# A two-layer hybrid encoder trunk: retention values in seven wide products, sums of weights on VectorE, other transfers and pacing

## The chip, the cores and the metric

The kernel runs on one core of one Trainium2 chip. The metric is the device time of one execution in microseconds (us); lower is better. Engines are named as in the profile: PE is TensorE (matmul), PEld its weight loads, DVE is VectorE, ACT is ScalarE, POOL is GpSimd, SP is SyncE, which issues most of the weight loads. SBUF is the on-chip memory, PSUM the eight banks that TensorE writes.

## The reference

Inputs are x (1, 512, 1024), a per-layer embedding p, and weights of two layers. All of it is float32. Cut to what matters here:

```python
for i in range(DEPTH):                      # 2 layers
    h = rmsnorm(x, norm1_g[i])
    z = h @ w_in[i] + b_in[i]               # q/k/v/o/i/f of the mLSTM, q/k/v/g of the retention, two gates
    ...
    y_m = sigmoid(mo) * head_layernorm(mlstm(mq, mk, mv, ...), m_norm_g[i])
    rq4, rk4 = rope(rq), rope(rk) * R_DK ** -0.5      # 4 heads, dk = 256
    hr = retention(rq4, rk4, rv, log_gamma)           # rv: 4 heads, dv = 512
    y_r = silu(rg) * head_layernorm(hr, r_norm_g[i])
    x = x + (sigmoid(gm) * (y_m @ w_bm[i]) + sigmoid(gr) * (y_r @ w_br[i])) @ w_out[i]
    h2 = rmsnorm(x, norm2_g[i])
    x = x + square(relu(h2 @ w_ff1[i] + b_ff1[i])) @ w_ff2[i] + b_ff2[i]
    h3 = rmsnorm(x, norm3_g[i])
    x = x + sigmoid(h3 @ w_pe_gate[i]) * (p[i] @ w_pe[i])
return rmsnorm(x, final_g)
```

The retention of one head over 512 frames is computed as masked scores times values (`r_scores`, `r_attend`); the part of z that the change is about is rv, 2048 columns, 512 for each of four heads.

## The kernel before, in words

**Numbers.** Every float32 operand is split into a high part (ScalarE, a rounded copy, `split` L263) and a low part (VectorE, the difference, L264). A product takes three matmuls: high by high, high by low, low by high (`mm3` L378 to L380).

**Units.** Weights are streamed in units of 512 KB, in an order that `unit_list` writes out. A T8 unit is 128 output columns, 24 matmuls with 512 frames moving. A V unit is a quarter of 512 value columns: here the weights move and the activations stand, and four units make 96 matmuls 128x512 (`values`, L614, matmuls L630 to L632). A PAIR unit is 256 output columns by a Strassen-Winograd scheme: seven products of 12 matmuls 128x256 each, instead of eight (`run_pair`, L408; matmuls L427 to L429).

**A PAIR's pieces.** The products read three loaded pieces, A = (B11, t1), B = (B21, t2), C = (B22, t3), and a fourth, D = t4 = B21 + t2, that VectorE forms in B's raw buffer (L364). t1, t3 and t2 are sums of weight quarters that GpSimd's DMA queue forms in DRAM ahead of time, two steps each (copy, then accumulate), up to 1 MB each, for a group of up to four pairs (`sum_steps`, `step`, L308). The steps are issued at units given by `due` and each waits for a matmul of its time.

**Buffers.** `fill_raws` loads pieces into four raw buffers (a fifth while the retention stages last) from SP's queue; `prep_next` splits them, in order, into a ring of three high/low pairs (`PIECES`), and D into a ring of two. `READY` and `LOOK` say how far ahead of a product the pieces are prepared.

**PSUM of a pair.** Products P1, P6, P7 and P4 use bank "a", P2 "b", P5 and P3 "c". P1 is evacuated before P6 starts on "a", P6 before P7, P7 before P4. The order on TensorE is P1, P5, then P4 of the pair before (`flush`), P6, P2, P3, P7. In most stages ScalarE evacuates P1, P5, P6 and P4, and VectorE P2, P3 and P7 (`pair_tiles`, L455, L459, L461); in the feed-forward block all go to VectorE and are added to x there (L1215, L1217). A list scheduler fixes the final order on each engine; it may move instructions against the program's order.

**Retention stages.** For each head: `r_qk` (two pairs, then rope on VectorE, L936 to L938), `rv_vals`, `r_scores`, `r_attend`, head norm, and `r_out` (two gate pairs and transposes). `values` adds the bias on VectorE (L598) and splits the result (L612). Behind w_out, x is loaded again for the residual, from ScalarE's queue (L1165).

Of the kernel before, what the change touches and what calls it, by code (L numbers as in the profile page):

```python
# [35 lines left out]
F32 = mybir.dt.float32  # L36
F32R = mybir.dt.float32r
# [5 lines left out]
P = 128  # L43
T = 512
# [50 lines left out]
MADE = {"t1": ("B12", "B11"), "t3": ("B12", "B22"), "t2": ("t1", "B22")}  # L95
# [4 lines left out]
def due(k):  # L100

    return 3 + 7 * min(k, 15) // 4 + 9 * max(k - 15, 0) // 4


def groups():


    g = {}
    for i in range(L):
        def rqk(h):  # L110
            return [("w_in", 0, c + k * 256) for k in (h, h + 1) for c in (CRQ, CRK)]
# [12 lines left out]
    return g  # L124


def unit_list(i):
# [48 lines left out]
    v(CRV)  # L176
# [6 lines left out]
    v(CRV + 512)  # L183
    rg(0)
    rqk(2)
    v(CRV + 1024)
# [3 lines left out]
    v(CRV + 1536)  # L190
# [23 lines left out]
def build(ctx, tc, ins, out):  # L214
# [29 lines left out]
    bm_dram = tc.dram_tile([L, KT, P, T], F32, name="bm_spill")  # L244

# [27 lines left out]
    index, given, sums, k = {}, {}, {}, 0  # L273
    for g, v in groups().items():
        index[g] = len(index)
        for x in GIVEN:
            given[g, x] = ins["wpairs"][k:k + len(v)]
            k += len(v)
        for x in MADE:
            sums[g, x] = tc.dram_tile([len(v), P, Q], F32, name=f"s{index[g]}{x}")  # L280
# [7 lines left out]
    def sum_steps():  # L288

        first = lambda g: [(g, "t1", 0), (g, "t3", 0), (g, "t1", 1), (g, "t3", 1)]  # L290
        second = lambda g: [(g, "t2", 0), (g, "t2", 1)]
        gs = list(index)
        out = first(gs[0])
        for a, b in zip(gs, gs[1:]):
            f = first(b)
            for n, x in enumerate(second(a)):
                out += [x] + f[2 * n:2 * n + 2]
        return out + second(gs[-1])
# [12 lines left out]

    def next_unit():
        n = at["unit"]
        at["unit"] += 1
        while at["step"] < len(steps) and due(at["step"]) <= n:
            step()
        return n


    order = [(n, x) for n, u in enumerate(units) for x in (PIECE if u[0] == "PAIR" else (0,))]  # L320
    place = {x: k for k, x in enumerate(order)}
    loads = [(n, x) for n, x in order if x != "D"]
    raws, pieces = {}, {}
# [3 lines left out]
    at = {"unit": 0, "prep": 0, "load": 0, "whole": 0, "step": 0}  # L327

    def fill_raws(most=RAWS + 1):
        while at["load"] < len(loads) and len(raws) < most:  # L330
# [8 lines left out]
            if x:  # L339
                _, g, p = units[n]  # L340
                assert made[g] == 6, (g, made[g], at["unit"])
                for k, y in enumerate(PIECE[x]):
                    in_order("load", nc.sync.dma_start(r[:, k * Q:(k + 1) * Q], block(g, y)[p]))
            else:
                in_order("load", nc.sync.dma_start(r, ins["wstream"][at["whole"]]))
                at["whole"] += 1
            at["load"] += 1

    def prep_next():
# [8 lines left out]
        out_ = [pl.tile([P, w], F32R, name=f"w{a}{n}_{x}", **kw) for a in "hl"]  # L358
        r = raws.pop((n, "B" if x == "D" else x))
        in_order("prep", *split(r[:, :w], *out_))  # L360
        pieces[n, x] = out_
        if x == "B":

            ve.tensor_tensor(r[:, :Q], r[:, :Q], r[:, Q:], OP.add)  # L364
            raws[n, x] = r
# [42 lines left out]
    def run_pair(name, act, done):  # L408
# [33 lines left out]
        later.append(last)  # L442

# [352 lines left out]
    for i in range(L):  # L796
# [166 lines left out]
        def r_out(h, num, y):  # L963
            nm = f"l{i}r{h}o"
            gs = {}

            def gates(w):
                def consume(g):
                    for d in range(2):
                        ac.activation(g[d], g[d], AF.Silu, bias=bcol(i, "brg", 4 * h + 2 * w + d), scale=SIGN[d])  # L970
                        gs[2 * w + d] = g[d]

                return consume

            for w in range(2):
                pair_tiles(f"{nm}{w}", xs, gates(w))
# [41 lines left out]

        def rv_vals(h, mid=None):
            return values(i, f"l{i}r{h}", xn, None, bias_rows(1024 + h * 512), 1, mid)  # L1020
# [99 lines left out]
        vv = rv_vals(3)  # L1120
# [43 lines left out]
        for c in range(KT):  # L1164
            nc.scalar.dma_start(x[c], x_src[c])  # L1165
# [184 lines left out]
    assert at["unit"] == NU and at["prep"] == len(order) and not pieces and not raws and at["load"] == len(loads) and at["step"] == len(steps)  # L1350
# [3 lines left out]
def _pack_units(a):  # L1354
# [7 lines left out]
    for i in range(L):  # L1362
        for u in unit_list(i):
# [3 lines left out]
            elif u[0] == "PAIR":  # L1367
# [15 lines left out]
def _pack_pairs(a):  # L1383

    out = []
    for (i, _), g in groups().items():
# [3 lines left out]
    return np.ascontiguousarray(np.concatenate(out))  # L1390
# [73 lines left out]
```

## Time and profile before

| what | value |
|---|---|
| median of three runs | 2360.72 us |
| the three runs | 2360.53 to 2361.47 us |
| the profiled execution, its own time | 2361.21 us |
| its span from first to last instruction | 2359.5 us |
| bytes read and written in HBM | 396.72 and 134.22 MB |

The prediction shows lines of the profile. In the page's list of engines stand busy time, share of the span and number of instructions; in the 40 slices each digit is the busy share in tenths. A row of the timeline has start, duration, engine, line, operation, what it writes and reads, and in brackets how long the engine was idle before it and for whom. A row of the view of waits has the waiting instruction, whom it waited for, the sum in us, how often, and the longest. A row of groups has minimum, median and maximum duration in ns and the first and last start. Matmuls are pipelined, so their durations overlap; the step from one start to the next is what one costs.

### The profile page before, as it was taken

The numbers are of one execution on the slowest core, as the hardware profiler recorded it, in microseconds if no ns is written. First come the engines' busy times: TensorE is split into PE (matmuls) and PEld (weight loads), VectorE is DVE, ScalarE is ACT, GpSimd is POOL, SyncE is SP. The second block draws the span as 40 slices with busy tenths as digits, with TensorE's granted clock in tenths as the row PEclk, the third lists the DMA queues.
The fourth block names the chain that finished last, engine by engine and source line by source line (L and its number), as shares of the span: only waits on it lengthen the run. The fifth ranks groups of instructions, "written<-read, shape, count | busy, mean of one in ns | idle before, by whom it ended". The sixth has DMA issues, their size and how long they took to land. (4 is left out here: it accounts for less than half of the span.)

```text
span 2359.5 us, 35353 instructions
## 1 busy us (share of the span) xinstructions
PE 2341.2 (99%) x13788; PEld 2077.1 (88%) x13788; DVE 1623.0 (69%) x2511; ACT 1194.0 (51%) x1736; POOL 232.2 (10%) x340
## 2 busy tenths in 40 slices
PE   9999999999999999999999999999999999999998
PEld 7888898998998898899888888999989988998997
DVE  6877567774675677677768775677837656776675
ACT  5755344553553545445557563444526445455454
POOL 4111100000001100001311110000000010000012
PEclk9999999999999999999999999999999999999999
DMA  6655765557577666765665657756574853433441
GB/s 217 172 173 159 208 211 161 179 157 224 156 230 253 181 197 192 196 179 161 189 187 160 165 174 210 195 183 167 170 219 159 243 178 99 143 125 116 135 133 55
DMA packets 156263, 413.71 MB, mean 175 GB/s; under 512 B 15664, under 2 KB 18096, under 8 KB 156096
## 3 DMA queue, kind: packets, MB, share of 16 engines
q1 hardware_dynamic: 107568, 260.32, 33.2%
q0 software_dynamic: 31104, 119.55, 21.6%
q10 hardware_dynamic: 17424, 31.59, 3.8%
q8 instruction: 108, 1.77, 0.3%
q14 instruction: 59, 0.48, 0.1%
HBM read 396.72 MB, written 134.22 MB: 225 GB/s over the span
## 5 line engine op out<-in xcount | busy, mean ns | idle before, releaser
L263 ACT ACTIVATE wh<-wr 128x1024 fp32r<-128x1024 f32 x254 | 268.1, 1057 | 383.7 <-issue 64.1
L264 DVE TENSOR_TENSOR wl<-wr,wh 128x1024 fp32r<-128x1024 f32 x254 | 311.4, 1227 | 137.4 <-ACT wh L263 131.3
L263 ACT ACTIVATE wh_C<-wr 128x1024 fp32r<-128x1024 f32 x76 | 80.5, 1059 | 130.5 <-PE l0bm L379 13.0
L264 DVE TENSOR_TENSOR wl_B<-wr,wh_B 128x1024 fp32r<-128x1024 f32 x76 | 92.9, 1222 | 44.5 <-ACT wh_B L263 39.5
L263 ACT ACTIVATE wh_B<-wr 128x1024 fp32r<-128x1024 f32 x76 | 80.4, 1057 | 84.0 <-issue 15.2
L263 ACT ACTIVATE wh_A<-wr 128x1024 fp32r<-128x1024 f32 x76 | 80.1, 1054 | 76.3 <-PE l1f L379 11.3
L264 DVE TENSOR_TENSOR wl_A<-wr,wh_A 128x1024 fp32r<-128x1024 f32 x76 | 92.9, 1222 | 33.1 <-ACT wh_A L263 33.1
L264 DVE TENSOR_TENSOR wl_C<-wr,wh_C 128x1024 fp32r<-128x1024 f32 x76 | 92.8, 1221 | 17.3 <-ACT wh_C L263 17.3
L378 PE MATMUL l1f<-l1n2h,wh 128*128 128x512 f32 x256 | 99.8, 390 | 0.0
L378 PE MATMUL l0f<-l0n2h,wh 128*128 128x512 f32 x256 | 99.8, 390 | 0.0
L380 PE MATMUL l0f<-l0n2h,wl 128*128 128x512 f32 x256 | 99.7, 389 | 0.0
L380 PE MATMUL l1f<-l1n2h,wl 128*128 128x512 f32 x256 | 99.7, 389 | 0.0
L379 PE MATMUL l0f<-l0n2l,wh 128*128 128x512 f32 x256 | 99.6, 389 | 0.0
L379 PE MATMUL l1f<-l1n2l,wh 128*128 128x512 f32 x256 | 99.6, 389 | 0.0
L263 ACT ACTIVATE wh_D<-wr 128x512 fp32r<-128x512 f32 x76 | 47.6, 627 | 93.6 <-PE l1o32a L428 3.5
L264 DVE TENSOR_TENSOR wl_D<-wr,wh_D 128x512 fp32r<-128x512 f32 x76 | 52.1, 686 | 45.6 <-ACT wh_D L263 44.5
L380 PEld LDWEIGHTS l1f<-l1n2h,wl 128*128 128x128 f32 x256 | 48.0, 188 | 10.2
L380 PEld LDWEIGHTS l0f<-l0n2h,wl 128*128 128x128 f32 x256 | 48.0, 188 | 10.1
L378 PEld LDWEIGHTS l0f<-l0n2h,wh 128*128 128x128 f32 x256 | 48.1, 188 | 9.8
L378 PEld LDWEIGHTS l1f<-l1n2h,wh 128*128 128x128 f32 x256 | 48.1, 188 | 9.8
L379 PEld LDWEIGHTS l0f<-l0n2l,wh 128*128 128x128 f32 x256 | 48.1, 188 | 9.8
L379 PEld LDWEIGHTS l1f<-l1n2l,wh 128*128 128x128 f32 x256 | 48.1, 188 | 9.7
(5493 smaller groups left out, 8255.4 us busy)
## 6 DMA issues: line engine op xcount, KB each, us to landing
wr<-wstream SPq DMA_DIRECT2D x254, 512.0 KB, 4.6
wr<-wpairs SPq DMA_DIRECT2D x228, 256.0 KB, 3.5
s0t<-wpairs POOLq DMA_DIRECT2D x5, 1024.0 KB, 8.6
s2t<-wpairs POOLq DMA_DIRECT2D x5, 1024.0 KB, 8.4
s3t<-wpairs POOLq DMA_DIRECT2D x5, 1024.0 KB, 8.6
s4t<-wpairs POOLq DMA_DIRECT2D x5, 1024.0 KB, 8.5
s5t<-wpairs POOLq DMA_DIRECT2D x5, 1024.0 KB, 8.7
s6t<-wpairs POOLq DMA_DIRECT2D x5, 1024.0 KB, 9.0
```

The costliest lines, as they stand in the source:

```text
L263: a = ac.activation(hi_ap, src, AF.Copy)
L264: return a, ve.tensor_sub(lo_ap, src, hi_ap.bitcast(F32))
L378: te.matmul(o, sh, mh, start=first, stop=False)
L379: te.matmul(o, sh, ml, start=False, stop=False)
L380: cur["mm"] = te.matmul(o, sl, mh, start=False, stop=last)
```

## The change

1. **Retention values.** Two heads' values are made together as a unit WIDE (groups rv0 and rv2, `run_wide`): seven products of 24 matmuls 128x512 instead of 2 x 96. Weights move, in halves u0 and u1 of 512 KB; the activations are the operands that the pairs use already. There are 12 loads (B11, t1, t2, B21, t3, B22, two halves each), 14 splits, and t4 = t2 + B21 by VectorE, one instruction of 1024 columns for each half. Each product is evacuated by VectorE in two tiles. The first head's values are split at once; the second head's go to DRAM by GpSimd's queue (four of 256 KB) and are loaded again and split by `rv_load`.
2. **t2 of the pairs.** t2 = t1 + B22 is formed by VectorE in SBUF when piece C is prepared (76 instructions of 512 columns), not by DMA. The pieces are prepared in the order A, C, B, D; the raw buffer of A is kept until t2 is formed. A group of pairs needs four DMA steps instead of six, a pair five loads of 256 KB instead of six.
3. **Pace.** The DMA steps are issued by a credit that grows with each unit (`tick`) instead of by `due`.
4. **Order.** A head's first gate pair is pulled ahead into a place that the values had (`r_gates`).
5. **x.** The reload for the residual goes by GpSimd's queue instead of ScalarE's.

```diff
-PIECE = {"A": ("B11", "t1"), "B": ("B21", "t2"), "C": ("B22", "t3"), "D": ()}
+PIECE = {"A": ("B11", "t1"), "C": ("B22", "t3"), "B": ("B21",), "D": ()}
...
+WIDE = {"P1": ("B11", 0), "P5": ("t1", 4), "P6": ("t2", 5), "P2": ("B21", 2), "P7": ("t3", 3), "P3": ("B22", 6),
+        "P4": ("t4", 1)}
+
+TURNS = [(x, u) for x in ("P1", "P5") for u in range(2)] + [(x, u) for u in range(2) for x in ("P6", "P2")]
+TURNS += [(x, u) for x in ("P7", "P3", "P4") for u in range(2)]
+STEP, SHARE = 4.5, 0.7
+TIME = {"PAIR": (9.9, 3.9), "WIDE": (5.45, 2.7)}
...
-def due(k):
-
-    return 3 + 7 * min(k, 15) // 4 + 9 * max(k - 15, 0) // 4
...
+        g[i, "rv0"] = [("w_in", 0, CRV)]
+        g[i, "rv2"] = [("w_in", 0, CRV + 1024)]
...
-    v(CRV)
+    u.append(("WIDE", (i, "rv0"), 0))
     full("w_bm", 0, 0, 0, 4)
     rqk(0)
     for p in (2, 3):
         pair("gm", p - 2)
         full("w_bm", 0, 0, 2 * p, 2 * p + 2)
     rqk(1)
-    v(CRV + 512)
     rg(0)
+    u.append(("WIDE", (i, "rv2"), 0))
     rqk(2)
-    v(CRV + 1024)
     rg(1)
     rqk(3)
     full("w_br")
-    v(CRV + 1536)
     rg(2)
     rg(3)
...
+    def tick(kind=None):
+        t, load = TIME.get(kind, (5.45, 1.5))
+        at["credit"] += SHARE * t - load
+        while at["step"] < len(steps) and at["credit"] >= 0:
+            at["credit"] -= STEP * len(groups()[steps[at["step"]][0]]) / 4 if not is_wide(steps[at["step"]][0]) else STEP
+            step()
...
-        if x == "B":
+        if x == "A" or wide and x[0] == "t2":
+            kept[n, x] = r
+        elif x == "C":
+
+            ve.tensor_tensor(raws[n, "B"][:, Q:], kept.pop((n, "A"))[:, Q:], r[:, :Q], OP.add)
+        elif x == "B":
 
             ve.tensor_tensor(r[:, :Q], r[:, :Q], r[:, Q:], OP.add)
-            raws[n, x] = r
+            formed[n, "D"] = r
+        elif wide and x[0] == "B21":
+            t = cur["br"].tile([P, UN], F32, name=f"t4{n}_{x[1]}", tag=("ph", "pl")[x[1]])
+            ve.tensor_tensor(t, kept.pop((n, ("t2", x[1]))), r, OP.add)
+            formed[n, ("t4", x[1])] = t
...
+    def run_wide(name, act, done, mid=None):
...
+            b = {"P2": "b", "P5": "c", "P3": "c"}.get(x, "a")
+            first = x in ("P1", "P2", "P5")
+            if first and u == 0:
+                bank[b] = [ps(f"{name}{b}{t}") for t in range(2)]
+            ready(place[n, (y, u)] + LOOK)
+            wh, wl = pieces.pop((n, (y, u)))
+            for k in (2 * u, 2 * u + 1):
+                h, l = act[k](j)
+                s = slice(k % 2 * T, (k % 2 + 1) * T)
+                f, e = first and k == 0, k == 3
+                for t in range(2):
+                    ts = slice(t * P, (t + 1) * P)
+                    o = bank[b][t]
+                    te.matmul(o, h[:, ts], wh[:, s], start=f, stop=False, skip_group_check=True)
+                    te.matmul(o, h[:, ts], wl[:, s], start=False, stop=False, skip_group_check=True)
+                    cur["mm"] = te.matmul(o, l[:, ts], wh[:, s], start=False, stop=e, skip_group_check=True)
+            if u:
+                for t in range(2):
+                    done(x, t, bank[b][t])
...
+        def rv_load(h):
+
+            v = value_tiles(f"l{i}r{h}")
+            for j in range(NT):
+                t = tmp(f"l{i}r{h}vr{j}")
+                gp.dma_start(t, rv_dram[i, h // 2, j])
+                split(t, v[0][j][:, :T], v[1][j][:, :T])
+            return v
...
         num = r_attend(0, pt, vv)
-        vv = rv_vals(1)
+        gs = {}
+        r_gates(0, 0, gs)
+        vv = rv_load(1)
         pt = r_scores(1, qk)
         yr = acts(cur["br"], f"l{i}yr0")
-        r_out(0, num, yr)
+        r_out(0, num, yr, gs)
         num = r_attend(1, pt, vv)
+        vv = rv_vals(2)
         qk = r_qk(2)
-        vv = rv_vals(2)
+        gs = {}
+        r_gates(1, 0, gs)
         pt = r_scores(2, qk)
-        r_out(1, num, yr)
+        r_out(1, num, yr, gs)
...
-        vv = rv_vals(3)
+        vv = rv_load(3)
...
-            nc.scalar.dma_start(x[c], x_src[c])
+            gp.dma_start(x[c], x_src[c])
```

More of the change, by code (lines that the diff above doesn't have):

```diff
@@ L288, in sum_steps @@
     def sum_steps():
[L290 to L298, printed above, removed]
+        out = []
+        for g in index:
+            out += [(g, "t1", 0), (g, "t3", 0), (g, "t1", 1), (g, "t3", 1)]
+            if is_wide(g):
+                out += [(g, "t2", 0), (g, "t2", 1)]
+        return out
     steps = sum_steps()
@@ L1349, in build @@
     x_pool.release()
-    assert at["unit"] == NU and at["prep"] == len(order) and not pieces and not raws and at["load"] == len(loads) and at["step"] == len(steps)
+    assert at["unit"] == NU and at["prep"] == len(order) and not pieces and not raws and at["load"] == len(loads) and not kept and not formed and at["step"] == len(steps)
 def _pack_units(a):
@@ L1366, in _pack_units @@
                 put(a[nm][i, r:r + D, c:c + P])
-            elif u[0] == "PAIR":
+            elif u[0] in ("PAIR", "WIDE"):
                 continue
```

136 lines of the change are left out of this document (104 added, 32 removed).

## The prediction

> **What bounds the kernel now.** I read the page first, for the share of each engine and whether it changes along the span, then the clock, the view of waits for TensorE, and single stretches in the timeline.
>
> ```profile
> span 2359.5 us, 35353 instructions
> PE 2341.2 (99%) x13788; PEld 2077.1 (88%) x13788; DVE 1623.0 (69%) x2511; ACT 1194.0 (51%) x1736; POOL 232.2 (10%) x340
> PE   9999999999999999999999999999999999999998
> DVE  6877567774675677677768775677837656776675
> core 0: 2359.5 us, clock 0.998
> ```
>
> TensorE is busy in every slice, at a granted clock of 0.998. The other engines are not near their limits on average, but VectorE stands at 7 or 8 tenths in many slices. What TensorE waits for is little:
>
> ```profile
> PE l0o33a L427 <- DVE l0x L1217: 2.0, 2, 1.5
> PE l1o33a L427 <- DVE l1x L1217: 2.0, 2, 1.5
> PE l1n41rp L572 <- DVE l1n41d L570: 1.6, 1, 1.6
> PE l0m0vp L631 <- DVE wl L264: 1.4, 1, 1.4
> PE warm L786 <- POOL ones_r L252: 1.1, 1, 1.1
> ```
>
> These rows and the smaller ones behind them come to about 10 us in 2359. So the time is the sum of TensorE's matmuls, and a change counts by the matmuls that it removes less the new gaps that it opens. The retention values, pairs of the feed-forward product and the retention stages all run without a gap now, which is why each new wait costs its full length.
>
> **What is removed.** The values of two retention heads take 2 x 96 matmuls of 512 columns before, and 7 x 24 = 168 of the same form after: 24 fewer for each of four pairs of heads, 96 in all. The instruction order shows nothing else leaving TensorE.
>
> ```profile
> L630 PE MATMUL l0r1vp<-wh,l0xnh x32: 389/389/389, 387.1 to 408.2; 128*128 128x512 f32 x32
> ```
>
> This row is every third matmul of one head. From its first to its last start there are 31 steps of three, 93 matmuls in 21.1 us: 0.227 us each (389 ns is the overlapping, modelled duration). 96 x 0.227 = 21.8 us. [...]
>
> **What VectorE is given.** Its pitches, from neighbouring starts:
>
> ```profile
> 939.15 1.22 DVE L264 TENSOR_TENSOR wl_B<-wr,wh_B 128x1024 fp32r<-128x1024 f32 x1 [0.55 <-ACT wh_B L263]
> 940.29 0.41 DVE L1217 TENSOR_TENSOR l0x<-l0x,l0o11c 128x256 f32<-128x256 f32 x1
> 940.63 0.68 DVE L364 TENSOR_TENSOR wr<-wr 128x512 f32<-128x512 f32 x1
> 941.23 0.41 DVE L1217 TENSOR_TENSOR l0x<-l0x,l0o11a 128x256 f32<-128x256 f32 x1
> 941.93 1.22 DVE L264 TENSOR_TENSOR wl_C<-wr,wh_C 128x1024 fp32r<-128x1024 f32 x1 [0.29 <-ACT wh_C L263]
> 943.08 0.41 DVE L1217 TENSOR_TENSOR l0x<-l0x,l0o12a 128x256 f32<-128x256 f32 x1
> 940.84 1.06 ACT L263 ACTIVATE wh_C<-wr 128x1024 fp32r<-128x1024 f32 x1 [1.72 <-PE l0o11a L428]
> 940.75 0.28 PE L427 MATMUL l0o12a<-l0hh,wh_A 128*128 128x256 f32 x1
> 943.58 0.28 PE L427 MATMUL l0o11a<-l0hh,wh_D 128*128 128x256 f32 x1
> ```
>
> A split of 1024 columns takes 1.14, a sum of 512 takes 0.60, an evacuation of 256 takes 0.34. New are 76 sums t2 (45.6 us). A wide unit has 14 splits and two t4 sums of 1024 columns, 14 evacuations and four value splits of 512: 16 x 1.14 + 18 x 0.60 = 29.0 us, and the reloaded head's four splits elsewhere are 2.4; before, two heads took 8 x 1.14 + 16 x 0.60 = 18.7. Four pairs of heads: 4 x 12.7 = 51 us. With these 97 us VectorE goes from 69% to about 73%: no new bound by its mean. What matters is where these instructions stand in its queue.
>
> **The new wait between two pairs.** In the rows above a pair (l0o12) starts at 940.75, call it 0. Piece C of the new pair takes the buffer that P7 of the old pair has just left, so ScalarE's wh_C starts at 0.09 and wl_C at 1.18. Before, the evacuations of the old P3 and P7 (940.29 and 941.23) stand ahead of wl_C. The old pair's P4, at 2.83 (943.58), writes the same PSUM bank as P7, so it needs that evacuation. In the changed order, piece C is prepared second and wl_C stands ahead of the old P3 and P7 evacuations on VectorE. Then: wl_C 1.18, evacuations at 2.33 and 2.67, the latter's end 2.67 + 0.41 = 3.08, P4 at 3.11 (0.03 is the step from wh_C's end to wl_C) instead of 2.83: 0.28. Next late is wl_B, 3.01 to 4.23, and behind it the evacuation of the new P1, 4.15 to 4.56; P6 shares P1's bank and wanted 3.11 + 1.41 = 4.52: 0.07 more. Together 0.35 us for each pair-to-pair change of this kind. Where the next t2 sum also stands between wl_C and the P7 evacuation, 0.60 is added, and the sum is about 1.0.
>
> Following the changed order for a layer's feed-forward blocks: of nine changes from pair to pair in blocks 0 to 2, three have the P7 evacuation early enough (0), five are of the first kind (1.75), one (second to third pair of block 0) is of the second (1.0). Block 3, where VectorE is already what TensorE waits for (the l0o33a row), I put at 0. That is 2.75 us per layer. Between pairs with a T8 unit in between (merge gates) P4 is late anyway and the cover is 2.7 us of T8 matmuls: 0; without them each would cost 0.35.
>
> **The retention stages.** Before, they ran at these shares:
>
> ```profile
> core 0: us, PE busy (x) PEld busy (x) DVE busy (x) ACT busy (x) POOL busy (x), PEclk, DMA share, GB/s
> 387.00:408.40 21.40, 21.40 (x96) 17.72 (x95) 12.37 (x22) 5.67 (x7) 3.03 (x4) 1.00 0.63 178
> 409.00:460.00 51.00, 51.00 (x395) 49.38 (x394) 39.94 (x67) 31.36 (x52) 2.48 (x4) 1.00 0.50 163
> ```
>
> The value unit (first stretch, 58% of VectorE) was the place where rope and norm work could catch up; the pair stage (78%) was the dense one. After, the values of heads 1 and 3 are not there to catch up in, and a wide unit of 168 x 0.227 = 38.1 us itself wants 29 us. The pair stretch from r_qk(2) to r_qk(3) has, counted in the changed order, 61 us of VectorE in 73 us of TensorE. By hand, per layer: the chain r_qk(0) to the second gm pair 2.0 (t2 stands waiting for piece C's load, 3.5 us or more after the slot is freed); r_qk(1) 0.35; P4 of the first gate pair behind head 0's norm and rope 0.6; r_qk(2)'s first change 0.8; the scores of head 2 waiting for the last k split 0.8; P4 of the last r_gates(1) pair 0.8 (between 0 and 1.6, as wl_C comes before or after P7's end); r_qk(3) 0.3; r_gates(2), where the scores, four value splits and a t2 precede the evacuations, 1.1; r_gates(3) 0.6; the two wide units 0.5 each. Sum 8.35. Each lies between 0, if the queue runs a little ahead, and about double. Places that I did not follow, and the second layer's own order: 0 to 2 us per layer, taken as 1, since nothing there can shorten TensorE's work.
>
> **Transfers.**
>
> ```profile
> wr<-wstream SPq DMA_DIRECT2D x254, 512.0 KB, 4.6
> wr<-wpairs SPq DMA_DIRECT2D x228, 256.0 KB, 3.5
> s2t<-wpairs POOLq DMA_DIRECT2D x5, 1024.0 KB, 8.4
> q0 software_dynamic: 31104, 119.55, 21.6%
> L1165 ACTq DMA_DIRECT2D l0x<-xT x8: 335/339/412, 719.1 to 734.5; - x8
> L308 POOL DMA_DIRECT2D s9t<-wpairs x5: 548/869/905, 823.1 to 951.2; - x5
> ```
>
> A wide unit loads 12 x 512 KB in 38 us, one per 3.2 us against 4.6 to land with four or more buffers: hidden; with only one buffer ahead it would cost 1.4 a piece. Groups of pairs need four DMA steps instead of six, so the pacing has room: by the code the last step of any group is issued at least five units (27 us or more) ahead of its first use, against some 9 us that a 1 MB step takes; 0. The eight reloads of x go behind each other on GpSimd, eight issues of 0.9 = 7 us instead of 0.34 each, ahead of the eight evacuations of w_out, which come 5.44 us apart (24 x 0.227): hidden, else about 5 us per layer. Spills and reloads of the second head have some 30 us: 0. [...]
>
> **Sum.** Per layer 2.75 + 8.35 + 1 = 12.1; two layers 24.2. Against the profiled execution: 2359.5 - 21.8 + 24.2 = 2361.9 span, plus the 1.7 between its span and its time (2361.21); that execution is 0.5 above the median of 2360.72, so about 2363 for the median. The whole saving is given back.
>
> **Rivals.** (1) *The waits stay covered*, and only the feed-forward changes remain, which follow from rows alone: 2 x 2.75, plus 3 for the rest. 2360.7 - 21.8 + 8.5 = 2347. For it: the stretch at 78% ran without a gap. Against: its evacuations stood ahead of the splits. (2) *VectorE becomes the bound in the wide units*, slower: 29 us of its own work and 8 to 12 of norm and rope of the neighbouring head meet in 38 us; above 38, each wide unit's splits come late turn after turn, as the ring of three pieces allows no lead. At 42 a wide unit costs 4 more, 16 for four: 2363 + 16 = 2379. It decides from a VectorE share of about 95% there. (3) *The matmuls saved are not saved time*: if the pitch of the wide unit were longer than 0.227 because weights change every four rows. Four units have 672; at 0.01 us more for each, 6.7 is not saved: 2370. Against: form and order of three per product are those of the values before.
>
> **How the numbers follow.** Forecast 0.5 (2354 to 2373), rival 1 0.25, rival 2 0.15, rival 3 0.05, others (a late sum or reload, slower) 0.05. About 0.2%, 4.7 us, is what a measurement can tell: below 2356 is faster, above 2365.4 slower. Rival 1 and a little of the forecast give faster 0.3; of the forecast, about 0.27 lies within; the rest, with rivals 2 and 3, slower 0.43, as unseen waits only add. Range: from rival 1's 2347 to rival 2's 2379.
>
> **What would show it.** TensorE instructions fall by 96, pitch in the wide unit 0.227. In the view of waits the new rows are first matmuls of P4 and P6 (tiles ending in "a") waiting for VectorE, 0.3 to 1 us each, some 30 us in all instead of 10. VectorE's share about 73%. Under 18 us in such rows makes rival 1 right; gaps inside the wide tiles, waiting for wl, make rival 2 right; waits for a DMA at piece loads, x or sums prove the part on transfers wrong.

## The result and the profile after

The changed kernel takes 2356.67 us (median of 20 runs, 2354.59 to 2359.66); the kernel before took 2361.14 us in the runs beside it (20 runs, 2360.43 to 2361.96). The ratio is 0.9982 (0.9976 to 0.9988): 4.5 us faster. Forecast were 2363 us and a range of 2347 to 2379. The time lies in the range, but the kernel became faster and not slower. Of the 21.8 us that the 96 matmuls are worth, 17.3 are given back, not 24.2.

From the page of the kernel after (span; engines with busy time, share and instructions; TensorE's tenths of 40 slices; clock):

```profile
span 2356.1 us, 35296 instructions
PE 2328.2 (99%) x13692; PEld 2062.1 (88%) x13692; DVE 1716.9 (73%) x2643; ACT 1217.9 (52%) x1760; POOL 252.3 (11%) x372
PE   9999999999999999999999999999999999999998
core 0: 2356.1 us, clock 0.997
```

13788 matmuls have become 13692, and VectorE stands at 73%, both as forecast. The slices show no gap. But the busy time of TensorE fell by 13.0 us (2341.2 to 2328.2), not by 21.8. Matmul records overlap, so this difference is no exact sum, but it suggests that something besides waiting got slower. The view of waits for TensorE, kernel after (who waited, for whom, total us, times, longest):

```profile
PE l0r2o1a L472 <- ACT wh_A L286: 4.4, 1, 4.4
...
PE l0r1brqa L472 <- DVE l0r1brqy L539: 1.4, 1, 1.4
...
PE l0r0o0a L472 <- DVE l0r0o0y L539: 1.2, 1, 1.2
```

All rows of this view add up to 20.5 us, against 11.5 before. One new row is far longer than any other: the second gate pair of head 2 in layer 0, waiting for piece A, and it has no counterpart in layer 1. To place the rest I took the step from each matmul's start to the next one's in the timeline, less 0.227 us for one of 512 columns and 0.118 for one of 256 (other widths in proportion), and summed this excess by the tile ahead of the step, before and after. The differences come to 18.2 us, against 18.4 from the spans (2359.5 - 21.8 = 2337.7; 2356.1 - 2337.7):

| place | excess, us |
|---|---|
| l0r2o, the pairs with the 4.4 us wait, layer 0 | +8.1 |
| P4 of the first gate pair of head 0, two layers | +2.8 |
| pitch inside the four wide units | +2.6 |
| l0r1br, q pair of head 1, layer 0 | +1.8 |
| first tile of bank c in a wide unit of layer 0 | +1.3 |
| l1r2o, layer 1 | +0.9 |
| l0m3, an mLSTM stage | +0.8 |
| feed-forward blocks 0 to 2, both layers, 0.1 to 0.4 at a place (l0o11 +0.3) | +2.0 |
| feed-forward block 3, both layers (l0o31 +1.0, l0o32 and l1o32 -0.8 each, the rest small) | -1.2 |
| all other places together | -0.9 |

**The 4.4 us wait.** The timeline of the kernel after, GpSimd, the ScalarE queue and ScalarE, then TensorE (start, duration, operation, in brackets the idle time before it and the releaser):

```profile
591.79 0.90 POOL L331 DMA_DIRECT2D s8t<-wpairs  x1 [9.98 <-DMA br_spill<-l0brs]
592.44 1.94 POOL L1147 DMA_DIRECT2D l0r3vr<-rv_spill  x3
602.05 0.54 POOL L1147 DMA_DIRECT2D l0r3vr<-rv_spill  x1 [7.67 <-issue]
592.74 0.33 ACTq L1252 DMA_DIRECT2D br_spill<-l0brs  x1
607.72 0.63 ACT L286 ACTIVATE l0r3vh<-l0r3vr 128x512 fp32r<-128x512 f32 x1 [1.88 <-DMA l0r3vr<-rv_spill]
608.26 1.04 ACT L286 ACTIVATE wh_A<-wr 128x1024 fp32r<-128x1024 f32 x1
609.35 0.55 PE L472 MATMUL l0r2o1a<-l0xnh,wh_A 128*128 128x256 f32 x1 [4.41 <-ACT wh_A L286]
```

Read it backwards. The matmul waits for wh_A, and wh_A stands on ScalarE behind the split of the fourth reloaded value tile. That tile was loaded only from 602.05, 7.67 us after the other three, and its row names no releaser ("issue"). In GpSimd's queue the four reloads stand behind a step of the sums (s8t, 1 MB). For that step and for the reloads, the view of their source line answers:

```profile
L331 POOL DMA_DIRECT2D s8t<-wpairs x1: 897/897/897, 591.8 to 591.8; - x1
DMA to landing us min/median/max: 9.9/9.9/9.9
L1147 POOL DMA_DIRECT2D l0r3vr<-rv_spill x4: 541/794/854, 592.4 to 602.1; - x4
DMA to landing us min/median/max: 5.6/10.7/11.6
```

591.79 + 9.95 = 601.74: the step lands, and 0.31 us later the last reload is issued. The same 0.31 to 0.32 stands between the two in each of the four other runs below that keep the reload on GpSimd's queue behind this step. By these runs it is not a buffer that it waits for. `rv_load` takes its temporaries from the six that `full("w_br")` spills from (l0brs), and the seventh of its eight spills, issued at 592.74 and slow too (8.8 us), also lands just ahead, at 601.5. But in the run with t2 by DMA the seventh spill lands at 599.2, the step at 607.91, and the last reload is issued at 608.22. In layer 1 no steps are left to issue by then, and there is no wait. The windows around the wait (us, busy us and count of PE, PEld, DVE, ACT, POOL, granted clock, DMA share, GB/s):

```profile
600.00:604.00 4.00, 4.00 (x36) 4.00 (x35) 1.90 (x3) 1.47 (x3) 1.10 (x2) 1.00 1.03 384
613.00:616.00 3.00, 3.00 (x16) 3.00 (x15) 1.52 (x2) 1.33 (x2) 0.00 (x0) 0.50 0.24 87
```

After the wait TensorE runs at a clock of 0.50 until about 616: 16 matmuls in 3 us, against 36 in 4 us ahead of it. The trace's record of the clock has 0.50 from 609.4 to 616.2. These 6.8 us do the work of 3.4: 28 matmuls of 256 columns start in them, 3.3 us at 0.118 each, and where nothing waits their step is 0.213. So the stall costs 4.4 + 3.4 = 7.8 of the 8.1 us at l0r2o, and this is where part of TensorE's busy time stayed. The page's mean clock, 0.997 after 0.998, hides it.

**The feed-forward change that came only in part.** The same change from l0o11 to l0o12 that the prediction counted out, timeline of the kernel after:

```profile
942.33 1.06 ACT L286 ACTIVATE wh_C<-wr 128x1024 fp32r<-128x1024 f32 x1 [1.11 <-issue]
943.42 1.22 DVE L287 TENSOR_TENSOR wl_C<-wr,wh_C 128x1024 fp32r<-128x1024 f32 x1
944.56 0.41 DVE L1350 TENSOR_TENSOR l0x<-l0x,l0o11c 128x256 f32<-128x256 f32 x1
945.22 0.42 DVE L1350 TENSOR_TENSOR l0x<-l0x,l0o11a 128x256 f32<-128x256 f32 x1 [0.24 <-PE l0o11a L474]
945.02 0.28 PE L472 MATMUL l0o12a<-l0hh,wh_A 128*128 128x256 f32 x1
947.85 0.28 PE L472 MATMUL l0o11a<-l0hh,wh_D 128*128 128x256 f32 x1
947.81 1.23 DVE L287 TENSOR_TENSOR wl_B<-wr,wh_B 128x1024 fp32r<-128x1024 f32 x1 [2.17 <-ACT wh_B L286]
948.96 0.42 DVE L1350 TENSOR_TENSOR l0x<-l0x,l0o12a 128x256 f32<-128x256 f32 x1
949.52 0.36 PE L472 MATMUL l0o12a<-l0hh,wh_B 128*128 128x256 f32 x1
```

And the first matmul of P6 in the kernel before, where the new pair starts at 940.75:

```profile
944.99 0.28 PE L427 MATMUL l0o12a<-l0hh,wh_B 128*128 128x256 f32 x1
```

wl_C does stand ahead of the evacuations of P3 and P7, as the instruction order had it. But wh_C starts at 942.33, before the new pair begins (945.02), because C, prepared second now, takes a buffer that came free earlier. VectorE is idle when P7 ends, the evacuation starts at 945.22, and P4 comes 2.83 us after the new pair's start, as before the change. The last link of the chain did come: wl_B goes ahead of the evacuation of the new P1, and P6, which needs P1's bank, starts 4.50 us after the new pair instead of 4.24. With the step behind it that is the 0.3 at l0o11.

### The profile page after: what moved, and what is told of

The parts are those of the page before. It is cut to its first block, busy times and chain, and to the rows that moved or that the text cites. A ratio compares the mean times of both kernels' runs of the same rounds, so it can differ in the third digit from the quotient of the medians.

```text
span 2356.1 us, 35296 instructions
## 1 busy us (share of the span) xinstructions
PE 2328.2 (99%) x13692; PEld 2062.1 (88%) x13692; DVE 1716.9 (73%) x2643; ACT 1217.9 (52%) x1760; POOL 252.3 (11%) x372
## 5 line engine op out<-in xcount | busy, mean ns | idle before, releaser
L286 ACT ACTIVATE wh<-wr 128x1024 fp32r<-128x1024 f32 x222 | 234.0, 1055 | 298.3 <-issue 64.9
L287 DVE TENSOR_TENSOR wl<-wr,wh 128x1024 fp32r<-128x1024 f32 x222 | 273.6, 1233 | 94.1 <-ACT wh L286 93.8
L286 ACT ACTIVATE wh_B<-wr 128x1024 fp32r<-128x1024 f32 x100 | 105.9, 1059 | 158.1 <-PE l0f L424 8.5
L287 DVE TENSOR_TENSOR wl_B<-wr,wh_B 128x1024 fp32r<-128x1024 f32 x100 | 122.1, 1221 | 31.0 <-ACT wh_B L286 30.8
L287 DVE TENSOR_TENSOR wl_A<-wr,wh_A 128x1024 fp32r<-128x1024 f32 x76 | 92.8, 1221 | 17.2 <-ACT wh_A L286 16.7
L402 DVE TENSOR_TENSOR wr<-wr,wr 128x512 f32<-128x512 f32 x76 | 52.2, 687 | 16.0 <-DMA wr<-wpairs 14.4
L425 PEld LDWEIGHTS l0f<-l0n2h,wl 128*128 128x128 f32 x256 | 48.0, 188 | 10.2
L425 PEld LDWEIGHTS l1f<-l1n2h,wl 128*128 128x128 f32 x256 | 48.0, 188 | 10.2
```

The lines of the kernel that those rows point to most:

```text
L286: a = ac.activation(hi_ap, src, AF.Copy)
L287: return a, ve.tensor_sub(lo_ap, src, hi_ap.bitcast(F32))
L402: ve.tensor_tensor(raws[n, "B"][:, Q:], kept.pop((n, "A"))[:, Q:], r[:, :Q], OP.add)
L425: cur["mm"] = te.matmul(o, sl, mh, start=False, stop=last)
```

## The experiments

Each edit is against the kernel after, unless it says otherwise. Ratios are to the kernel before, with 95% intervals.

**Reload by another queue.** Two kernels move the reload of the second head's values off GpSimd's queue, one to SyncE's, one to ScalarE's (the second has `nc.scalar` in the same place).

```diff
-                gp.dma_start(t, rv_dram[i, h // 2, j])
+                nc.sync.dma_start(t, rv_dram[i, h // 2, j])
```

> The second head's values are loaded again by SyncE's queue instead of GpSimd's; everything else as changed. Theory (queue): in layer 0 the reload of head 3 stands behind a 1 MB sum step in GpSimd's queue, lands 8 to 10 us after its issue, and ScalarE, in order, holds wh_A of the next gate pair behind it; that costs some 7 us on TensorE in the gate pairs of head 2 of layer 0 (excess over the matmuls' pitch 8.4 us there in layer 0 against 1.2 in layer 1). Then the time falls by 6 to 8 us, to about 2349.5, the 4.4 us wait is gone, and layer 1 is unchanged. Rival (work): the four extra splits and the second t2 sum in that place cost the time, whatever the queue: within 1.5 us of the changed kernel. A second rival: SyncE's queue then holds the weight loads behind the reload's own wait and new waits for wh or wl appear: slower than the changed kernel.

> The second head's values are loaded again by ScalarE's queue instead of GpSimd's. Theory (queue): the same gain as from SyncE's queue, 6 to 8 us, unless ScalarE's issue waits for the buffers that the spills of w_br leave; then ScalarE holds wh of a weight unit and 1 to 5 us come back. Rival (work): within 1.5 us of the changed kernel.

SyncE's queue: 2358.29 us, 0.9989 (0.9979 to 0.9999); ScalarE's: 2358.02 us, 0.9990 (0.9981 to 0.9999). Neither beats the change. The wait is still there, in each kernel's view of waits; on SyncE's queue:

```profile
PE l0r2o1a L472 <- ACT wh_A L286: 4.7, 1, 4.7
```

On SyncE's queue the four reloads are issued from 596.1 to 602.0 and take 8.6 to 8.8 us to land, beside the same step. On ScalarE's they are issued from 596.5 to 602.9, the last behind the split of the first, and the wait is 5.7, with another of 1.5 in layer 1. So another queue alone does not help. It does not clear GpSimd's queue in the kernel after: there the last reload is issued when the step has landed.

**No sum step beside the spills.** `tick` issues nothing during the eight w_br units of heads 0 and 1 (row block 0) and the unit behind them.

```diff
+        n = at["unit"] - 1
+        if any(units[m][0] == "T8" and units[m][1] == "w_br" and units[m][2] == 0 for m in (n, n - 1)):
+            return
```

> No sum step is issued during the eight w_br units of heads 0 and 1; the credit goes on and the steps come behind them. Buffers as in the changed kernel. Theory (DMA engines shared with a sum step): the spills land in 2 to 4 us as in layer 1, the last reload is issued some 5 us earlier, and layer 0's gate pairs of head 2 lose at most 2 us as in layer 1: 2349 to 2352. Rival (buffers alone, or work): the wait of 4.4 us stays, within 2 us of 2356.7.

2355.87 us, 0.9981 (0.9972 to 0.9991): no better than the change within the interval. Its reloads, the seventh spill, and its view of waits:

```profile
L1150 POOL DMA_DIRECT2D l0r3vr<-rv_spill x4: 536/554/606, 573.7 to 589.9; - x4
DMA to landing us min/median/max: 2.7/2.9/3.0
L1255 ACTq DMA_DIRECT2D br_spill<-l0brs x1: 326/326/326, 592.6 to 592.6; - x1
PE l0r2o1a L475 <- DVE l0r2o1y L542: 3.0, 1, 3.0
PE l0r3o1a L477 <- DVE wl_A L287: 1.9, 1, 1.9
```

The wait for wh_A is gone. The reloads are issued 12 to 19 us earlier, the last one ahead of the seventh spill (so it does not need that spill's buffer), and land in 3 us instead of 5.6 to 11.6. So the steps made the reload late: ahead of it in GpSimd's queue, and as a transfer beside it. But the steps held back now come behind each other, and two waits for VectorE stand at 623.5 and 643.9 us instead of the one at 609.4. After the 3.0 us wait the granted clock stays at 1.00.

**Reload into its own buffers.** The reload goes straight into the value tiles (the low part, split in place), and head 3's is issued ahead of `full("w_br")`. So no buffer is shared with the spills, and the reload goes ahead of the steps that stood ahead of it. The recorded texts call this kernel e6.

```diff
-                t = tmp(f"l{i}r{h}vr{j}")
-                gp.dma_start(t, rv_dram[i, h // 2, j])
-                split(t, v[0][j][:, :T], v[1][j][:, :T])
+                gp.dma_start(v[1][j][:, :T].bitcast(F32), rv_dram[i, h // 2, j])
+            return v
+
+        def rv_split(v):
+            for j in range(NT):
+                split(v[1][j][:, :T].bitcast(F32), v[0][j][:, :T], v[1][j][:, :T])
...
-        vv = rv_load(1)
+        vv = rv_split(rv_load(1))
...
+        vv = rv_load(3)
         for c in range(KT):
...
-        vv = rv_load(3)
+        vv = rv_split(vv)
```

> The reloaded head's values land in the value buffers themselves (the low part's, split in place), not in the six temporaries that the spills of w_br also use, and head 3's reload is issued before w_br. Moving the reload to another queue had changed nothing: the last reload was issued at 602.0 in both, just after a w_br spill that shared the DMA engines with a 1 MB sum step (issued at 591.8) had taken 8.8 us. Theory (shared temporaries): the reload then lands long before the scores of head 3, the 4.4 us wait of layer 0 and the half clock behind it go (7 to 8 us), and layer 1 stays: 2348 to 2350. Rival (work): the splits and sums that stand ahead on ScalarE and VectorE hold the gate pair: within 2 us of 2356.7.

2352.09 us (2350.11 to 2353.69), 0.9965 (0.9953 to 0.9978): 4.6 us below the change, faster than both kernels. Its issues in the view of the source line, and its window over the place of the stall:

```profile
L1146 POOL DMA_DIRECT2D l0r3vl<-rv_spill x4: 546/558/594, 532.6 to 534.7; - x4
```

```profile
604.00:616.00 12.00, 12.00 (x104) 12.00 (x103) 7.45 (x12) 7.02 (x13) 0.00 (x0) 1.00 0.61 206
```

The reloads are issued 60 us earlier, TensorE runs through at full clock, and the excess at l0r2o goes back to what it was before the change. The run does not separate the buffers from the earlier issue. The span falls by 5.5 (2356.1 to 2350.6) and not by 8. Two of the places that give some back are in its view of waits, where the kernel after had 1.2 each:

```profile
PE l0r0o0a L472 <- DVE l0r0o0y L539: 1.7, 1, 1.7
PE l1r0o0a L472 <- DVE l1r0o0y L539: 1.7, 1, 1.7
```

**Piece buffers strictly in turn.** This makes the prediction's assumption true: piece C of the new pair gets exactly the buffer that P7 of the old pair leaves.

```diff
-        out_ = [pl.tile([P, w], F32R, name=f"w{a}{n}_{nm}", **kw) for a in "hl"]
+        if kw["tag"] == "w":
+            turn = at["turn"] = at.get("turn", -1) + 1
+            out_ = [pl.tile([P, w], F32R, name=f"w{a}{n}_{nm}", tag=f"w{turn % PIECES}{a}", bufs=1) for a in "hl"]
```

> The three buffer pairs of the split pieces are taken strictly in turn, so that piece C of a pair must take the buffer of the last pair's piece C and wait for its P7, as the prediction assumed; in the changed kernel wh_C started at 942.33, before P7 (943.61 to 945.02) had begun. Theory (buffers): the prediction's chain then appears, about 0.35 us at each of some ten feed-forward changes from pair to pair and about 1 us at two of them, 5 to 6 us in all, and some more in the retention stages: 2361 to 2366 us. Rival: the chain is covered in any case, for example because the evacuation of P7 runs earlier than I chained it: within 1.5 us of the changed kernel's 2356.7.

2356.87 us, 0.9983 (0.9974 to 0.9992): no different. The same change of pairs in its timeline:

```profile
945.18 0.42 DVE L1354 TENSOR_TENSOR l0x<-l0x,l0o11a 128x256 f32<-128x256 f32 x1 [0.99 <-PE l0o11a L478]
946.21 1.23 DVE L287 TENSOR_TENSOR wl_C<-wr,wh_C 128x1024 fp32r<-128x1024 f32 x1 [0.60 <-ACT wh_C L286]
```

C does wait for P7 now, but the scheduler then puts the P7 evacuation ahead of wl_C. Where the buffer is late the order is the harmless one, and where the order is the harmful one the buffer is early. The order and the buffer were not independent, and the chain that joined them, through P7 to P4, does not stand at this change of pairs in either kernel.

**t2 formed later.** t2 is formed just ahead of B's split, so that it does not stand waiting for C's load.

```diff
         if x == "B":
+            ve.tensor_tensor(r[:, Q:], kept.pop((n, "A"))[:, Q:], kept.pop((n, "C"))[:, :Q], OP.add)
...
-
-            ve.tensor_tensor(raws[n, "B"][:, Q:], kept.pop((n, "A"))[:, Q:], r[:, :Q], OP.add)
+            kept[n, "C"] = r
```

> VectorE forms t2 just before piece B is split, not when piece C is prepared; pieces A and C keep their raw buffers until then. Theory: the t2 sum no longer stands ahead of wl_C and the evacuations while it waits for a load (4.09 us at the second pair of r_qk(1), layer 0), so the 1.4 us there and the 0.9 in layer 0's last feed-forward block go: 2 to 3 us less than 2356.7. Rival: two raw buffers are kept instead of one, so loads start later and weight splits wait: 2 to 10 us more, with new waits for wl or wh.

2359.80 us, 0.9998 (0.9988 to 1.0007): 3.1 slower than the change. The place aimed at did improve (l0r1br by 1.7), and l0r0o, l1r0o (1.5 each) and the merge gates of both layers got worse.

**t2 of the pairs by DMA again**, with all else as in the change, the pieces in the old order A, B, C, D, and the credit of a step cut to two thirds.

```diff
-PIECE = {"A": ("B11", "t1"), "C": ("B22", "t3"), "B": ("B21",), "D": ()}
+PIECE = {"A": ("B11", "t1"), "B": ("B21", "t2"), "C": ("B22", "t3"), "D": ()}
...
-            if is_wide(g):
-                out += [(g, "t2", 0), (g, "t2", 1)]
+            out += [(g, "t2", 0), (g, "t2", 1)]
```

> The pairs' t2 is formed by DMA steps again, with the pieces in the order A, B, C, D, six steps per group and the same credit per group; the wide units and everything else stay. Theory: of the 17.5 us given back, the t2 sums on VectorE hold about 3 (1.6 at the first change from pair to pair of r_qk(1) in layer 0, where t2 waited 4.09 us for a load, 1.0 in the last feed-forward block of layer 0), so 2353 to 2358 if the extra DMA steps do not delay the reloads further; the reload of head 3 stands behind more steps, so its stall stays or grows by 1 to 3 us. Rival (relief): the t2 sums relieve the DMA engines and pieces, and without them the time grows by more than 5 us, with waits for sums or loads in the view of waits.

2372.46 us (four runs), 1.0055 (1.0036 to 1.0073): 15.8 slower than the change. The wait at l0r2o1 is 7.8 there, and a new one of 4.5 stands in layer 1 at l1bgm. Its windows around the latter:

```profile
1292.00:1296.00 4.00, 0.46 (x3) 0.04 (x1) 4.00 (x17) 2.52 (x4) 0.22 (x2) 1.00 0.14 53
1298.00:1300.00 2.00, 2.00 (x6) 1.59 (x5) 1.84 (x5) 0.00 (x0) 0.72 (x2) 0.50 0.85 264
```

Again half the clock after a wait of over 4 us. VectorE is busy for all 4.00 us of the first window. Because the reload's stall distorts this comparison, it was made once more on the kernel with the reload in its own buffers, with the two-thirds credit up to the 40th step only:

> e6, but the pairs' t2 by DMA steps again (pieces in the order A, B, C, D, six steps a group, 2/3 of the credit each up to the 40th step and the full credit then, as the first groups are due early). It tells what the t2 sums on VectorE are worth without the reload's stall. Theory (the sums cost little and relieve the DMA engines): slower than e6 by 3 to 12 us, with waits spread over places where weights or spills land late (DMA at 9 tenths and more in many slices of layer 0). Rival (VectorE's order was what the saving was lost to): faster than e6 by 2 us or more.

2361.26 us, 1.0008 (0.9999 to 1.0018), against 2352.09 with t2 on VectorE: 9.2 us. 3.5 of these are the excess at l1bgm; the rest is spread (the first gate pairs of head 0, with 3.4 us at half clock in layer 0, and head 3's q pair in both layers, a wide unit of layer 1). The pieces' loads do land later than in e6 (median 4.2 us against 2.9, 456 MB moved against 396). But at l1bgm the wait is for a VectorE that is busy, while the DMA engines move nothing (window 1280 to 1284, shown further below); how it comes to that is not shown. Its view of waits:

```profile
PE l1bgm L421 <- DVE wl L287: 3.2, 1, 3.2
```

**t2 on VectorE alone**: the kernel before with only the second part of the change (t2 formed when C is prepared, order A, C, B, D, two steps fewer to a group).

```diff
-PIECE = {"A": ("B11", "t1"), "B": ("B21", "t2"), "C": ("B22", "t3"), "D": ()}
+PIECE = {"A": ("B11", "t1"), "C": ("B22", "t3"), "B": ("B21",), "D": ()}
...
+        elif x == "C":
+            ve.tensor_tensor(raws[n, "B"][:, Q:], kept.pop((n, "A"))[:, Q:], r[:, :Q], OP.add)
```

> The kernel before, with only the pairs' t2 on VectorE (order A, C, B, D, four steps a group, the steps spread by the old schedule at 3/2 of the spacing); the values stay in the old units. On the kernel with wide units, taking t2 off VectorE again cost 9 us (2361.3 against 2352.1). Theory (t2 only pays where the wide units make VectorE's and the DMA engines' time short): before the change there was little to gain, as TensorE waited 11.5 us in all, so within 2.5 us of the kernel before. Rival (t2 on VectorE pays by itself): 3 to 8 us faster than before. Rival (the sums disturb the order on VectorE, as the prediction had it): 3 to 8 us slower.

2364.36 us, 1.0015 (1.0006 to 1.0025): 3.5 us slower than the kernel before. Its VectorE is busy for 1668.9 us, 45.9 more than before, which is the 45.6 that the prediction gave the sums. The loss has no place: 0.2 to 0.6 at each of a dozen pairs, and 0.8 gained in each layer at l0o32 and l1o32. So part 2 alone loses 3.5, the rest without it (the run above) does not gain, and the two together, with the reload in its own buffers, are worth 8.2 (2360.33 to 2352.09).

**The activations' place in SBUF.** The kernel puts a spacer of 16 columns (64 bytes a partition) ahead of the operand sums xs. This leaves the spacers out. It ran once.

```diff
-        shift(xs_pool, act_side, True)
         xs_t = acts(xs_pool, f"l{i}xs")
-        shift(xs_pool, act_side, False)
```

> The sums of the activations (xs) lie 64 bytes lower: the small spacers around their pool are left out. In the changed kernel's wide unit, matmuls that have xs standing step at 0.2335 us and those that have xn standing at 0.2267. Theory (place in SBUF against the moving weights): with xs at the same offset as xn the wide unit's step becomes 0.227 throughout, 2.6 us less in four units, and the pairs, which move xs against standing weights, may slow by up to as much or more. Rival (the operand's shape): the 0.2335 stays, as do the pairs.

2357.81 us, a span of 2356.1, equal to that of the change. Groups of matmuls of the wide unit in which xs stands, first the kernel after, then this one (minimum, median and maximum duration in ns, first and last start):

```profile
L515 PE MATMUL l0r2va<-wh_t,l0xsh x16: 393/396/398, 452.6 to 468.6; 128*128 128x512 f32 x16
...
L515 PE MATMUL l0r2va<-wh_B,l0xnh x8: 389/389/389, 441.6 to 446.3; 128*128 128x512 f32 x8
```

```profile
L515 PE MATMUL l0r2va<-wh_t,l0xsh x16: 389/389/389, 452.1 to 467.7; 128*128 128x512 f32 x16
```

The stretch from first to last start has 69 steps (P6, P2 and P7, 72 matmuls, less three): 16.0 us against 15.6. In neighbouring starts the step with xs standing is 0.2334 with the spacer and 0.2268 without, which is the pitch that xn has in both. But in the pairs, where xs moves, the step goes from 0.118 to 0.120 without it. By one execution of each, the two about cancel.

**Gates not pulled ahead**, on the kernel with the reload in its own buffers: head 0's first gate pair goes back to its old place.

```diff
-        gs = {}
-        r_gates(0, 0, gs)
...
-        r_out(0, num, yr, gs)
+        r_out(0, num, yr)
```

> e6, but the first gate pair of head 0 is not pulled ahead of the scores of head 1; it comes behind them as before the change. In e6 its P4 waits 1.7 us for VectorE in each layer, behind head 0's norm and rope. Theory (density): VectorE's work at that place does not depend on the order, so the wait moves to the scores of head 1, which now come right behind r_attend(0) and need the k split, and grows: 2 to 8 us slower than e6's 2352.1. Rival: the pulled-ahead pair is itself the cause, and the two waits of 1.7 go: 2 to 4 us faster.

2358.00 us, 0.9994 (0.9985 to 1.0003): 5.9 slower than with the gates pulled ahead. In its view of waits the scores of head 1 wait for the last k split, and the gate pair waits none the less:

```profile
PE l0r1s L423 <- ACT l0r1kh L286: 2.4, 2, 2.2
...
PE l1r0o0a L472 <- ACT l1r0o0y L529: 2.0, 1, 2.0
```

Not all of the 5.9 is waiting. In each layer 3.4 us at half clock follow the gate pair's wait, which costs an estimated 1.5 each, by the steps of 0.213 and 0.118 us that the kernel after has at the two clocks. The window in layer 0:

```profile
421.30:424.50 3.20, 3.20 (x17) 3.20 (x16) 3.12 (x6) 2.79 (x4) 0.00 (x0) 0.50 0.33 87
```

**Both**: the reload in its own buffers and the piece buffers in turn.

> e6 (reload into the value buffers) and the three buffer pairs of pieces taken strictly in turn. The strict turn alone moved 2356.7 to 2356.9, but removed 1.0 in the last feed-forward block, 0.7 at r_qk(1) and 0.9 in each of the two gate stages at the layers' ends (l0pg, l1pg), against 0.5 more at the scores of head 1 in each layer. Theory: the two edits touch different places and add up: 2350 to 2352, at most 1.5 below e6's 2352.1. Rival: the order on VectorE changes with both, and new waits take their place: above 2353.

2351.75 us (2349.85 to 2353.71), 0.9965 (0.9953 to 0.9978): the same as with the reload alone. Either is the best version that was run.

## Why the prediction was right or wrong

**What is removed: right.** 96 matmuls fewer. At xn's pitch of 0.227 they are worth the 21.8 us.

**"The matmuls saved are not saved time" (rival 3): a longer pitch is real, at 2.6 of its 6.7 us, but not for the reason given.** "Form and order of three per product are those of the values before" left out that other data stand: with xs standing a step takes 0.2334. The run without spacers, where it takes 0.2268, shows that it is their place in SBUF, and not the weights changing every four rows, since xn has the same change at 0.227.

**The new wait between two pairs, 5.5 us: 2.0 measured in the blocks it was counted for.** The step that failed is "Piece C of the new pair takes the buffer that P7 of the old pair has just left". The order of VectorE that it was joined with was right. C's buffer is free earlier, wh_C starts 2.7 us before the new pair, and P4 is not late. What came at the change shown is the last link, P1's evacuation behind wl_B, put at 0.07 and worth 0.3. Block 3, put at 0, gains 1.2, so the feed-forward blocks cost 0.8 in all. The row of before that the chain was built on showed C as the third piece; the change makes it the second, and the buffer had to be counted again.

**The retention stages, 16.7 us for both layers: too high, 6.8 measured.** The terms were mis-sized in both directions. P4 of the first gate pair behind head 0's norm and rope was put at 0.6 and cost 1.4 a layer. VectorE's rows of the kernel after show why:

```profile
414.86 1.92 DVE L759 TENSOR_SCALAR l0r0num<-l0r0num,l0r0mv,l0r0hv 128x512 f32<-128x512 f32 x4 [1.26 <-POOL l0r0hv L1037]
...
417.29 1.22 DVE L287 TENSOR_TENSOR wl_A<-wr,wh_A 128x1024 fp32r<-128x1024 f32 x1
...
419.09 1.22 DVE L287 TENSOR_TENSOR wl_C<-wr,wh_C 128x1024 fp32r<-128x1024 f32 x1
420.22 0.42 DVE L539 TENSOR_TENSOR l0r0o0y<-l0r0o0a,l0r0o0y 128x256 f32<-128x256 f32 x1
```

VectorE stands idle for 1.26 us for GpSimd's hv, and then the norm, wl_A and wl_C go ahead of the evacuation. The prediction counted work that stands ahead, and not that VectorE would itself wait there. r_qk(1) was put at 0.35 a layer and cost 1.8 in layer 0 alone; there the t2 sum waits for a load:

```profile
389.36 0.69 DVE L402 TENSOR_TENSOR wr<-wr,wr 128x512 f32<-128x512 f32 x1 [4.09 <-DMA wr<-wpairs]
...
391.44 0.41 DVE L539 TENSOR_TENSOR l0r1brqy<-l0r1brqa,l0r1brqy 128x256 f32<-128x256 f32 x1
```

"t2 stands waiting for piece C's load" is the mechanism that the prediction had for r_qk(0), at another place. The wide units were put at 2.0 in all and have 1.3; r_gates(2) at 1.1 a layer has 0.9 in layer 1. The others (r_qk(2), the scores of head 2, the last r_gates(1), r_qk(3), r_gates(3)) came to nothing that the steps show. That the queue of VectorE runs ahead there, the low end that the prediction had named, is likely, but no run shows it. The places not followed, put at 2, came to 0.8 (l0m3), and all other places gain 0.9.

**Transfers: "Spills and reloads of the second head have some 30 us: 0" is wrong by 8.1 us,** the largest error of any one term. The time between spill and reload was looked at, and not when the reload can be issued and what runs beside it: three of the four go at 592.4, behind a 1 MB step in GpSimd's queue, and the last when that step has landed. That the steps are the cause is shown by the run without them, where the wait for wh_A is gone; that another queue is no way out, by the two runs on other queues (2358.29 and 2358.02 us). What the stall was worth in time, 4.6 us, is shown by the run with the earlier reload in its own buffers. That a late spill held the last temporary is not borne out: without the steps the last reload goes ahead of that spill. The prediction had "a late sum or reload" among its other cases, with a chance of 0.05. The sums in time, the x reload and the piece loads were as said, apart from r_qk(1)'s. A reload of x from another queue was not tried. One reading of the kernel before was a little off, and nothing hangs on it: its waits add up to 11.5 us, not about 10.

**t2 as a cost only: half right.** As the only edit it costs 3.5 us. In the changed kernel (with the reload in its own buffers) its absence costs 9.2. That the steps then crowd the loads, as the wide units bring steps of their own, is likely but shown only in part: the loads land later (median 4.2 us against 2.9), yet the longest new wait is for VectorE, and order and pace of the steps change with it. The prediction noted that groups need four steps instead of six, called it room and priced it at 0.

**The rivals.** Rival 1 (2347) had the feed-forward part, which fell, as the only cost; without the reload's stall the kernel comes to 2352, between it and the forecast. Its sign of under 18 us in the rows of waits was just missed by the kernel after (20.5). Rival 2 did not decide: over the wide unit of head 2, 441.5 to 480.4, VectorE is busy for 31.77 of 38.9 us, 82% against the 95% that it needed.

**The sum.** Forecast 5.5 + 16.7 + 2 + 0 + 0 = 24.2 for feed-forward changes, retention stages, places not followed, pitch and reload; measured 0.8 + 6.8 - 0.1 + 2.6 + 8.1 = 18.2. Two errors of opposite sign hid behind each other: small waits in VectorE's order, of which most did not come, and one transfer that was taken as hidden. That the time comes as near to the forecast as it does is luck. What stays open is why just these hand-counted chains were covered and not the others, and where in detail the 3.5 us of t2 alone go.

## What to carry to other kernels

For a moved or added transfer ask first when it can be issued: what stands ahead of it in its queue, and which large transfer runs beside it (with a 1 MB step ahead and beside, the reload took 5.6 to 11.6 us to land, without one 3). Time in hand between the spill and the reload is no answer to that, and another queue did not help while the large transfer ran (8.6 to 8.8 us to land on SyncE's). A chain of waits built on the order of one engine has to be checked against the buffer that starts it, since the list scheduler here changed the order when the buffer came later (the evacuation of P7 at 945.18, wl_C at 946.21). An edit that loses alone (3.5 us here) can be worth keeping beside another one (9.2): price it in the kernel that it goes into.

## What was not expected of the hardware

**Half the clock after a wait.** How long TensorE stands still does not alone decide what follows. After the 4.4 us of the kernel after, the granted clock is 0.50 for 6.8 us, and so it is after 4.5 us (t2 by DMA) and 3.5 us (t2 formed later). After waits of only 2.0 us (gates not pulled ahead, both layers) it is 0.50 for 3.4 us, and after the wait of 7.8 us with t2 by DMA for 10.2. But after 3.0 us, in the run without a step beside the spills, it stays at 1.00, and so it does after 3.2 us, in the run with t2 by DMA and the reload in its own buffers, as its windows show:

```profile
1280.00:1284.00 4.00, 0.76 (x5) 0.30 (x3) 3.93 (x15) 3.51 (x5) 1.22 (x2) 1.00 0.00 0
1284.00:1288.00 4.00, 4.00 (x18) 3.31 (x19) 2.86 (x6) 1.65 (x2) 2.00 (x2) 1.00 0.72 153
```

In the traces of the kernels before and after, each change of the clock comes a multiple of 3.413 us behind the run's first change to full clock: after, 0.50 begins at 177 times that length (609.42) and ends at 179 (616.25), and the 0.50 at the run's end begins at 686 times; before, it begins at 687 times. In the stretch of 3.413 us ahead of such a change to 0.50, TensorE stood still for 3.34 us (the wait) and 2.20 (the end) in the kernel after and for 2.05 in the kernel before; in no other such stretch at full clock did it in these two traces for more than 1.51 us. No run was made to test this. Why waits of 2.0 us were followed by half clock and those of 3.0 and 3.2 us were not is not shown.

**Where the operands lie.** The same matmul of 512 columns takes a step of 0.2334 us with the standing operand 64 bytes further on in SBUF and 0.2268 without the spacer, while pairs that move this operand take 0.118 and 0.120 (one execution of each). No run here shows the rule behind it.
